# Global attention's sums of weights dealt out anew between VectorE and GpSimd, with the neighbourhood tables and the maxima placed differently

## The chip, the core and the metric

The kernel runs on one core of a Trainium2 chip. The core has engines with a queue each, worked off in order: TensorE (PE; matrix products into PSUM), VectorE (DVE), ScalarE (ACT), GpSimd (POOL) and SyncE (SP), which here issues the DMAs. The metric is the device time of one execution in microseconds. Most executions agree within 0.3%.

## What is computed

Two layers of a diffusion backbone on 1024 latent tokens (a grid of 16 rows by 64 columns) and 256 context tokens, width 1024, all in float32. Each layer: modulated norm, one input projection, three groups of heads, each multiplied by its own SiLU gate, one output projection and a gated residual. Cut to what matters here:

```python
def dense_attn(q, k, v):                       # global heads: 8 query heads, 2 key heads
    s = jnp.einsum("bqkgd,bskd->bkgqs", q, k)
    p = jax.nn.softmax(s, axis=-1)
    return jnp.einsum("bkgqs,bskd->bqkgd", p, v)
# neighbourhood heads (4): a query sees 8 rows x 16 columns around it, and the context
s = jnp.concatenate([s_nb + bias, s_ctx], axis=-1)
p = jax.nn.softmax(s, axis=-1)
o = einsum(p_nb, v_nb) + einsum(p_ctx, v_ctx)
y = jnp.concatenate([a_out * silu(ag), b_out * silu(bg), n_out * silu(ng)], -1) @ w_out
```

In the last layer only the latent tokens are queries; in the first the context tokens are too.

## The kernel before

**Stages.** Per layer: input projection (with norms, rotary embedding and gates, the results kept in DRAM), neighbourhood attention, in the first layer the context's own attention, global attention, output projection. The order of TensorE's instructions is the program's. Those of the other engines are set by a scheduler that runs at build time: each queue takes in order of the program what is ready by then, so a later step can come ahead of one that still waits. Once built, each queue is fixed.

**Neighbourhood attention** works in units of two heads and 128 queries: 8 units per pair of heads and layer, 10 in the first layer, and there 8 context units more (`units`, 28 in the first layer and 16 in the last). A unit has scores (L850, L851), the table of relative positions added and the minimum taken on DVE (L857), weights on ScalarE (L870), the gate times the reciprocal on POOL (`rg`, L873), transposes on TensorE (L886) through three PSUM banks `ps_b`, and values (L898). While unit n scores, unit n-1 transposes and unit n-2 takes its values. The table of a head exists twice: `ntab` (T, by DMA and L777), and `itab` (I), for inner queries: L781 copies ten columns of T, L782 to L784 overwrite its three outer pieces with a large number. There are two buffers of each, so heads 2 and 3 patch again what heads 0 and 1 patched. `before`, filled by `early(i, fn)`, says ahead of which unit a load is issued: the next pair's keys and queries, tables, the keys of the global attention (`gk`, three DMAs and two POOL memsets, L766 and L767) and its first queries (`load`).

**Global attention** has 8 units per layer (chunk of 512 queries, key head, pair of heads), `gunits`, numbered 0 to 7. Softmax needs each query's maximum first. `shift` makes it in 20 steps per unit: one product into a `ps_b` bank (L1007, or two of half the size, L1012) and its maximum on DVE (L1008, L1013); a 21st, `shift_rows`, puts the maxima into the second query operand. Of these steps 29 are done during the neighbourhood attention, from unit `nun - n_shifts` on, three a unit; the others run between the products of the global attention, one unit and a little ahead. For each unit and each kp from 0 to 4 (256 keys): scores of head hi=0, a shift step, the values of the step before, a shift step or two, scores of hi=1, two shift steps. Behind each group of scores stands the exponential on ScalarE into `gp` (L1036). The sum of weights of one head is a running sum `gacc` (L1041, L1044) over the five `gp`; the first three adds run on POOL, the last (kp=4) on DVE, and L1046 folds its two halves there. `finish` (at kp=2 of the next unit) sums over partitions on TensorE (L1062), makes the reciprocal (ScalarE L1066, L1067; DVE L1069, L1070), multiplies by gate and values (POOL L1071, DVE L1072), and `store_u` splits the result into a rounded part (`hh`, ScalarE's cast, L819) and the rest (`hl`, DVE, L820). `gp` and `gacc` share 7 buffers.

From unit 7 on, TensorE has no shift steps left: those of the last unit end in unit 6.

Of the kernel before, what the change touches and what calls it, by code (L numbers as in the profile page):

```python
# [7 lines left out]
F32 = mybir.dt.float32  # L8
F32R = mybir.dt.float32r
BF16 = mybir.dt.bfloat16  # L10
AF = mybir.ActivationFunctionType
ALU = mybir.AluOpType
# [4 lines left out]
P = 128  # L17
# [10 lines left out]
FAR = 1e30  # L28
# [46 lines left out]
def hybrid_block_kernel(  # L75
# [8 lines left out]
    PE, ACT, DVE, POOL, SP = nc.tensor, nc.scalar, nc.vector, nc.gpsimd, nc.sync  # L84
# [40 lines left out]
    def ps_one(name):  # L125
        wide.b += 1
        return ps_b[wide.b % 3]
# [250 lines left out]
    for l in range(DEPTH):  # L378
        last = l == DEPTH - 1
# [61 lines left out]
        def silu_to(dst, ps, n, s=None):  # L441
            s = s or wp.tile([P, 512], F32, name="sig", bufs=2)
            sigmoid(s[:, :n], ps)
            DVE.tensor_tensor(out=dst, in0=ps, in1=s[:, :n], op=ALU.mult)
# [48 lines left out]
        if l:  # L493
# [3 lines left out]
            for i in range(2):  # L497
                pr = ps_pair("ps_feat")
# [97 lines left out]
        for t in range(ntq):  # L596
            ps = proj_tok(W, t, 256)
            g = wp.tile([P, 512], F32, name="gate", bufs=2)
# [132 lines left out]
        def gate_out(ps, f, t0, n, s=None):  # L731
            g = s or wp.tile([P, 512], F32, name="gate", bufs=2)
            silu_to(g, ps, 512, s)
            SP.dma_start(out=agd[f, :, t0:t0 + n], in_=g)
# [15 lines left out]

        tab_bufs = [(ak_.tile([P, 14, 64], F32, name=f"ntab{i}"), ak_.tile([P, 10, 64], F32, name=f"itab{i}")) for i in range(2)]

        def kst():
            return ak_.tile([P, NT], F32R, name="kst", bufs=6)

# [6 lines left out]
        def load_gk(g):  # L762

            k1, k2 = load_twice(kst(), kad, g, 1), kst()
            SP.dma_start(out=k2[64:128].bitcast(F32), in_=head(kad, g, 0, slice(0, NT)))
            POOL.memset(k2[0:64].bitcast(F32), 0.0)  # L766
            POOL.memset(k2[0:1].bitcast(F32), 1.0)  # L767
            return k1, k2
# [9 lines left out]

        def na_inner(h):
            T, I = tab_bufs[h % 2]  # L780
            ACT.activation(out=I, in_=T[:, 2:12], func=AF.Copy)  # L781
            POOL.memset(I[0:64, 8:10], FAR)  # L782
            POOL.memset(I[64:128, 0:1], FAR)
            POOL.memset(I[64:128, 9:10], FAR)  # L784

        def load_nq(h, c0, n):
            t = ak_.tile([P, 512], F32R, name="nq", tag="q", bufs=QB)
# [13 lines left out]
        def na_q(pr, cc):  # L801
            cur["q", pr, cc] = [load_nq(2 * pr + hi, cc * 512, 512 if cc < 2 else 256) for hi in range(2)]
# [7 lines left out]
            g()  # L810


        def store_u(f, t0, n, u, eng=DVE):

            dst = hh[:, f, t0:t0 + n]
            if eng is POOL:
                POOL.tensor_copy(out=dst, in_=u)
            else:
                ACT.activation(out=dst, in_=u, func=AF.Copy)  # L819
            eng.tensor_tensor(out=hl[:, f, t0:t0 + n], in0=u, in1=dst.bitcast(F32), op=ALU.subtract)  # L820
# [86 lines left out]
        units, before = [], {}  # L907
# [3 lines left out]
        def early(i, fn):  # L911
            before.setdefault(max(i, 0), []).append(fn)

        order = [0, 1, 6, 7, 4, 5, 2, 3] + list(range(NTL, ntq))
        for pr in range(2):
            s0 = len(units)
            units += [("n", pr, t) for t in order]
            early(s0, lambda pr=pr: na_q(pr, 1))
            if not last:
                early(s0 + 4, lambda pr=pr: na_q(pr, 2))  # L920
            if pr == 0:
                for i, fn in enumerate(na_keys_load(1)):
                    early(s0 + 1 + i * (len(order) - 2) // 8, fn)
                for h in range(2):
                    early(s0 + 5 + h, lambda h=h: na_table(2 + h))
                early(len(units) - 1, lambda: na_q(1, 0))
                for h in range(2):
                    early(len(units) + 1 + h, lambda h=h: na_inner(2 + h))
            else:
                early(s0 + 4, lambda: gk(0))  # L930
        if not last:
            for g in range(2):
                for pr in range(2):
# [39 lines left out]
        def gk(g):  # L973
            if g not in gks:
                gks[g] = load_gk(g)
            return gks[g]


        def ga_unit(cc, g, pr):
            f = 2 * g + pr  # L980
            cs = slice(cc * 512, (cc + 1) * 512)
            st = _Env()
# [35 lines left out]
            def shift_rows():  # L1018
# [5 lines left out]
                for hi in range(2):  # L1024
                    SP.dma_start(out=st.q2[hi][0:1, :].rearrange("o (i p) -> o i p", p=P).bitcast(F32),
                                 in_=r[4 * hi:4 * hi + 4, :].bitcast(F32))

            def scores(hi, kp):
                k1, k2 = gk(g)
                S = ps_pair("ps_st").rearrange("p (a b) -> p a b", a=2)  # L1030
                for i in range(2):
                    kc = slice((2 * kp + i) * P, (2 * kp + i + 1) * P)
                    PE.matmul(S[:, i, :], k1[:, kc], st.q1[hi], start=True, stop=False)  # L1033
                    PE.matmul(S[:, i, :], k2[:, kc], st.q2[hi], start=False, stop=True)  # L1034
                p = ap_.tile([P, 2, 512], F32, name="gp", tag="prob", bufs=PB)
                ACT.activation(out=p, in_=S, func=AF.Exp)  # L1036
                st.p[hi, kp] = p
                pf = p.rearrange("p a b -> p (a b)")
                if kp == 1:
                    st.acc[hi] = ap_.tile([P, 1024], F32, name="gacc", tag="prob", bufs=PB)  # L1040
                    POOL.tensor_tensor(out=st.acc[hi], in0=st.p[hi, 0].rearrange("p a b -> p (a b)"), in1=pf, op=ALU.add)  # L1041
                elif kp > 1:
                    eng = DVE if kp == 4 else POOL
                    eng.tensor_tensor(out=st.acc[hi], in0=st.acc[hi], in1=pf, op=ALU.add)  # L1044
                if kp == 4:
                    DVE.tensor_tensor(out=st.acc[hi][:, 0:512], in0=st.acc[hi][:, 0:512], in1=st.acc[hi][:, 512:1024], op=ALU.add)  # L1046

            def values(kp, i):
                if kp == 0 and i == 0:
# [9 lines left out]
            def finish():  # L1059
                s_ps = ps_one("ps_gs")  # L1060
                for hi in range(2):
                    PE.matmul(s_ps[hi * 64:(hi + 1) * 64, :], ones, st.acc[hi][:, 0:512], start=True, stop=True)  # L1062
                gt = ap_.tile([P, 512], F32, name="ggate", tag="fin", bufs=4)
                SP.dma_start(out=gt, in_=agd[f, :, cs])
                r0 = ap_.tile([P, 512], F32, name="gr0", tag="fin", bufs=4)
                ACT.activation(out=r0, in_=s_ps, func=AF.Ln)  # L1066
                ACT.activation(out=r0, in_=r0, func=AF.Exp, scale=-1.0)  # L1067
                t1 = ap_.tile([P, 512], F32, name="gt1", tag="fin", bufs=4)
                DVE.tensor_tensor(out=t1, in0=s_ps, in1=r0, op=ALU.mult)  # L1069
                DVE.scalar_tensor_tensor(out=t1, in0=t1, scalar=-2.0, in1=r0, op0=ALU.add, op1=ALU.mult)  # L1070
                POOL.tensor_tensor(out=gt, in0=gt, in1=st.osb, op=ALU.mult)  # L1071
                DVE.scalar_tensor_tensor(out=t1, in0=t1, scalar=-1.0, in1=gt, op0=ALU.mult, op1=ALU.mult)  # L1072
                store_u(f, cc * 512, 512, t1)

            return shift, scores, values, finish, load, shift_rows

        gunits = [ga_unit(cc, g, pr) for cc in range(2) for g in range(2) for pr in range(2)]

        shifts = []
        for i, u in enumerate(gunits):  # L1080
# [1 line left out]
            shifts += own[:2] + ([gunits[i - 1][5]] if i else []) + own[2:]  # L1082
        shifts.append(gunits[-1][5])
        for i in range(2):
            early(len(units) - 12, gunits[i][4])

        use_banks("pair")
        env.att = False
# [3 lines left out]
        last_gate = 3, 512, 512  # L1092
        ps_gate = proj_feat(W, *last_gate, ps_acc)
# [3 lines left out]
        ap_ = attx.enter_context(pool(f"attp{l}", side=right))  # L1097
        prev = [None, None]
        nun = len(units)
        n_shifts = 7 if last else 10  # L1100
        n_ahead = 21 + GA_AHEAD

        def shift_step(n, least=0):
            for _ in range(n):
                if len(shifts) > least:
                    shifts.pop(0)()

        n_all = len(shifts)
        for n, u in enumerate(units + [None, None]):
            for fn in before.get(n, ()):  # L1110
                fn()
            fns = (make_unit(*u) if n else first) if u else None
            p1, p2 = prev
            for hi in range(2):
                if fns and n:
                    fns[0](hi)
                if p1:
                    p1[2](hi)
                if fns:
                    fns[1](hi)  # L1120
                if hi == 0 and n >= nun - n_shifts:
                    shift_step(1, n_all - n_ahead)
            shift_step(2 if n >= nun - n_shifts else 0, n_all - n_ahead)
            if n == 1:

                gate_out(ps_gate, *last_gate, tab_bufs[0][1].rearrange("p a k -> p (a k)")[:, 0:512])
            if p2:
                p2[3]()
            prev = [fns, p1]
            env.att = True  # L1130
# [38 lines left out]
        op = opx.enter_context(pool(f"op{l}", side=left))  # L1169
# [48 lines left out]
        for t0, n in ochunks:  # L1218
# [4 lines left out]
            for i in range(n):  # L1223
# [13 lines left out]
                elif last and t == NTL - 1:  # L1237

                    for c0, w in ((0, 512), (512, 256), (768, 256)):
                        ps, cs = ps_one("ps_y"), slice(c0, c0 + w)  # L1240
                        for k in range(KT):
                            a, b = hh[:, k, ts_], hl[:, k, ts_]
# [7 lines left out]
                else:  # L1250
                    ps, f = proj_out(t)
# [88 lines left out]
```

## Time and profile before

| what | us |
|---|---|
| median of the runs shown (3, from 1533.07 to 1533.96) | 1533.53 |
| profiled execution | 1532.11 |
| its span in the profile | 1530.3 |
| neighbourhood and context attention, first layer | 383 to 505 |
| global attention, first layer | 505 to 722 |
| neighbourhood attention, last layer | 1117 to 1219 |
| global attention, last layer | 1219 to 1436 |
| TensorE busy in the span | 1468.8 |

A row of the timeline has the start, the duration, engine, line, operation, out<-in, sizes and count; in brackets the time that the engine stood idle before it and what ended that. In a row of waits stand the waiting instruction, what it waited for, the total, how often and the longest. A row of stretches has for each engine the busy time and, in brackets, the instructions, in the order PE, PEld (weight loads), DVE, ACT, POOL, then the granted share of TensorE's clock, the share of the DMA engines, and GB/s.

### The profile page before, as it was taken

What the parts mean: (1) busy time and instruction counts of PE and PEld (TensorE: products, weight loads), DVE (VectorE), ACT (ScalarE), POOL (GpSimd) and SP (SyncE); (2) the same over time, 40 slices, a digit from 0 to 9 for tenths busy, and PEclk for the clock granted to TensorE, in tenths of its full rate; (3) what the DMA queues carried; (4) which work ended last, traced back from release to release, by engine and by line L of the source; (5) the groups of instructions that cost most, each with busy time, mean ns of one, the idle gap of its engine ahead of it and who ended that gap; (6) DMA issues with size and microseconds to landing.
All of it is one profiled execution on the core that took longest, in us unless ns stands there. A gap on an engine that the chain in (4) does not pass through costs nothing.

```text
span 1530.3 us, 22281 instructions
## 1 busy us (share of the span) xinstructions
PE 1468.8 (96%) x8001; PEld 1071.0 (70%) x8001; DVE 863.9 (56%) x1666; ACT 636.8 (42%) x1220; POOL 515.5 (34%) x630
## 2 busy tenths in 40 slices
PE   5999999999999999999999999999998999999999
PEld 3787777788887554544788888878787755544577
DVE  3545345542778678774533552464368878785522
ACT  4543232343776444444312452332466544444400
POOL 0243346000243565564001323460014265665300
PEclk9999999999999999999999999999999999999999
DMA  9447445437745101010522232343696201011331
GB/s 318 141 140 229 127 151 168 140 111 187 180 128 151 56 22 42 22 42 21 179 75 98 61 114 71 90 138 88 174 223 157 87 22 42 21 28 35 137 118 55
DMA packets 153040, 167.91 MB, mean 110 GB/s; under 512 B 35385, under 2 KB 112033, under 8 KB 152865
## 3 DMA queue, kind: packets, MB, share of 16 engines
q1 hardware_dynamic: 152928, 166.48, 37.0%
q8 instruction: 63, 1.03, 0.3%
q14 instruction: 49, 0.39, 0.1%
HBM read 126.45 MB, written 40.86 MB: 109 GB/s over the span
## 4 chain that ended last, share of the span: by engine, by line
PE 80%; DVE 8%; ACT 4%; DMA 4%; issue 3%; SPq 1%; POOL 0%; DVEq 0%; ACTq 0%; POOLq 0%
PE ps_c L1053 8%; PE ps_w L423 8%; PE ps_w L422 8%; PE ps_w L424 8%; PE ps_w L1208 4%; PE ps_w L1211 4%; PE ps_w L1209 4%; PE ps_w L1033 4%; PE ps_b L1007 4%; PE ps_c L898 3%; PE ps_w L1034 3%; PE ps_b L886 2%; PE ps_w L430 2%; PE ps_w L432 2%; PE ps_w L431 2%
## 5 line engine op out<-in xcount | busy, mean ns | idle before, releaser
L1036 ACT ACTIVATE gp<-ps_w 128x1024 f32<-128x1024 f32 x160 | 162.4, 1021 | 194.3 <-PE ps_w L1034 158.7
L422 PE MATMUL ps_w<-wh,hh 128*128 128x512 f32 (+1 forms) x624 | 234.7, 376 | 1.9 <-ACT wh L291 1.9
L423 PE MATMUL ps_w<-wl,hh 128*128 128x512 f32 (+1 forms) x624 | 228.6, 366 | 1.1 <-DVE wl L292 0.9
L424 PE MATMUL ps_w<-wh,hl 128*128 128x512 f32 (+1 forms) x624 | 228.1, 365 | 0.0
L1008 DVE TENSOR_REDUCE gmx<-ps_b 128x1 f32<-128x512 f32 x256 | 171.8, 685 | 73.5 <-PE ps_b L1007 69.3
L1053 PE MATMUL ps_c<-gp,av 128*64 128x512 f32 x640 | 169.3, 621 | 10.3 <-ACT gp L1036 10.3
L1044 POOL TENSOR_TENSOR gacc<-gacc,gp 128x1024 f32<-128x1024 f32 x64 | 161.3, 2547 | 25.8 <-ACT gp L1036 25.5
L422 PEld LDWEIGHTS ps_w<-wh,hh 128*128 128x128 f32 x624 | 117.7, 189 | 25.8 <-issue 2.9
L423 PEld LDWEIGHTS ps_w<-wl,hh 128*128 128x128 f32 x624 | 117.5, 188 | 21.8 <-DVE wl L292 2.8
L424 PEld LDWEIGHTS ps_w<-wh,hl 128*128 128x128 f32 x624 | 117.3, 188 | 21.1
L1034 PE MATMUL ps_w<-gq,kst 128*128 128x512 f32 x320 | 126.2, 395 | 0.0
L1208 PE MATMUL ps_w<-woh,hh 128*128 128x512 f32 x272 | 109.4, 402 | 0.0
L643 DVE TENSOR_REDUCE qss<-sq 128x8 f32<-128x512 f32 (+2 forms) x58 | 31.2, 538 | 136.2 <-ACT sq L641 136.2
L1209 PE MATMUL ps_w<-wol,hh 128*128 128x512 f32 x272 | 107.5, 395 | 0.0
L1053 PEld LDWEIGHTS ps_c<-gp,av 128*64 128x64 f32 x640 | 43.3, 138 | 89.4 <-issue 66.5
L1041 POOL TENSOR_TENSOR gacc<-gp 128x1024 f32<-128x1024 f32 x32 | 75.8, 2369 | 50.2 <-ACT gp L1036 50.2
L292 DVE TENSOR_TENSOR wl<-wraw,wh 128x512 fp32r<-128x512 f32 (+1 forms) x96 | 66.6, 713 | 37.4 <-ACT wh L291 35.9
L1211 PE MATMUL ps_w<-woh,hl 128*128 128x512 f32 x272 | 85.6, 395 | 0.0
L430 PE MATMUL ps_w<-hh,wh 128*128 128x512 f32 (+1 forms) x208 | 80.3, 386 | 1.3 <-ACT wh L291 1.3
L870 ACT ACTIVATE prob<-ps_w,m 128x768 f32<-128x768 f32 (+2 forms) x88 | 72.7, 826 | 20.6 <-DVE m L857 7.4
L432 PE MATMUL ps_w<-hh,wl 128*128 128x512 f32 (+1 forms) x208 | 78.6, 378 | 0.0
L431 PE MATMUL ps_w<-hl,wh 128*128 128x512 f32 (+1 forms) x208 | 78.0, 375 | 0.0
(225 smaller groups left out, 2914.8 us busy)
## 6 DMA issues: line engine op xcount, KB each, us to landing
wmod<-in_w_mod_dram SPq DMA_DIRECT2D x48, 512.0 KB
wraw<-in_w_in_dram SPq DMA_DIRECT2D x64, 256.0 KB
gq<-qad SPq DMA_DIRECT2D x64, 128.0 KB
woraw<-in_w_out_dram SPq DMA_DIRECT2D x14, 512.0 KB
wraw<-in_w_in_dram SPq DMA_DIRECT2D x48, 128.0 KB
kst<-knd SPq DMA_DIRECT2D x16, 320.0 KB
qad<-qklo SPq DMA_DIRECT2D x18, 256.0 KB
qad<-qkhi SPq DMA_DIRECT2D x18, 256.0 KB
```

The source lines that it names most:

```text
L422: PE.matmul(ps[:, :n], a, wh[:, off:off + n], start=(k == 0), stop=False)
L423: PE.matmul(ps[:, :n], a, wl[:, off:off + n], start=False, stop=False)
L424: PE.matmul(ps[:, :n], b, wh[:, off:off + n], start=False, stop=(k == KT - 1))
L430: PE.matmul(ps[:, :n], wh[:, fs], hh[:, k, ts_], start=(k == 0), stop=False)
L1008: DVE.reduce_max(out=mx[:, qt, half:half + 1], in_=S, axis=AX.X)
L1034: PE.matmul(S[:, i, :], k2[:, kc], st.q2[hi], start=False, stop=True)
L1036: ACT.activation(out=p, in_=S, func=AF.Exp)
L1044: eng.tensor_tensor(out=st.acc[hi], in0=st.acc[hi], in1=pf, op=ALU.add)
L1053: PE.matmul(st.o[hi * 64:(hi + 1) * 64, :], av[:, kt, g * 64:(g + 1) * 64], st.p[hi, kp][:, i, :], start=(kt == 0), stop=(kt == NTT - 1))
L1208: PE.matmul(ps[:, i2, :], a, oh[:, cs], start=(k == 0), stop=False)
L1209: PE.matmul(ps[:, i2, :], a, ol[:, cs], start=False, stop=False)
L1211: PE.matmul(ps[:, i2, :], b, oh[:, i2 * 512:(i2 + 1) * 512], start=False, stop=(k == KT - 1))
```

## The change

It has three parts.

*Who adds.* `add_eng` names the engine of each add of weights by unit n, head hi and kp. In units 0 to 5 the add of kp=4 stays on DVE for hi=0 and goes to POOL for hi=1, with its folding. In unit 6 DVE has the adds of kp=4 and that of hi=1, kp=3; in unit 7 it has all of hi=1 and kp=4 of hi=0. In units 5 and 6 `store_u` casts on DVE instead of ScalarE.

*Tables.* The outer pieces of both `itab` buffers are set once per layer, as the buffers are made, and `na_inner` copies the inner pieces alone, by two ScalarE instructions (64 partitions by 512 columns each). The last gate of the projection, which used the first `itab` as scratch, takes a tile of its own.

*Maxima.* The 29 early steps start at the 15th unit from the end instead of the 10th in the first layer (12th instead of 7th in the last), at two a unit instead of three (in the last layer two and three by turns). For that `gk(0)` is loaded ahead of unit 5 (first layer) or 3 (last) instead of unit 14 or 9 (there the first early step asks for it, ahead of the entry for unit 12), and the first two units' queries ahead of unit 11 or 2 instead of 16 or 4.

```diff
+        for T, I in tab_bufs:
+            POOL.memset(I[0:64, 8:10], FAR)
+            POOL.memset(I[64:128, 0:1], FAR)
+            POOL.memset(I[64:128, 9:10], FAR)
...
         def na_inner(h):
             T, I = tab_bufs[h % 2]
-            ACT.activation(out=I, in_=T[:, 2:12], func=AF.Copy)
-            POOL.memset(I[0:64, 8:10], FAR)
-            POOL.memset(I[64:128, 0:1], FAR)
-            POOL.memset(I[64:128, 9:10], FAR)
+            ACT.activation(out=I[0:64, 0:8], in_=T[0:64, 2:10], func=AF.Copy)
+            ACT.activation(out=I[64:128, 1:9], in_=T[64:128, 3:11], func=AF.Copy)
...
-        def store_u(f, t0, n, u, eng=DVE):
+        def store_u(f, t0, n, u, eng=DVE, cp=None):
             dst = hh[:, f, t0:t0 + n]
-            if eng is POOL:
-                POOL.tensor_copy(out=dst, in_=u)
+            if eng is POOL or cp:
+                (cp or eng).tensor_copy(out=dst, in_=u)
             else:
                 ACT.activation(out=dst, in_=u, func=AF.Copy)
...
-                early(s0 + 4, lambda: gk(0))
+                early(s0 - 5, lambda: gk(0))
...
+            def add_eng(hi, kp):
+                if n == 7:
+                    return DVE if hi or kp == 4 else POOL
+                if n == 6:
+                    return DVE if kp == 4 or (hi and kp == 3) else POOL
+                return DVE if kp == 4 and hi == 0 else POOL
...
                 if kp == 1:
-                    POOL.tensor_tensor(out=st.acc[hi], in0=st.p[hi, 0].rearrange("p a b -> p (a b)"), in1=pf, op=ALU.add)
+                    add_eng(hi, kp).tensor_tensor(out=st.acc[hi], in0=st.p[hi, 0].rearrange("p a b -> p (a b)"), in1=pf, op=ALU.add)
                 elif kp > 1:
-                    eng = DVE if kp == 4 else POOL
+                    eng = add_eng(hi, kp)
                     eng.tensor_tensor(out=st.acc[hi], in0=st.acc[hi], in1=pf, op=ALU.add)
                 if kp == 4:
-                    DVE.tensor_tensor(out=st.acc[hi][:, 0:512], in0=st.acc[hi][:, 0:512], in1=st.acc[hi][:, 512:1024], op=ALU.add)
+                    eng.tensor_tensor(out=st.acc[hi][:, 0:512], in0=st.acc[hi][:, 0:512], in1=st.acc[hi][:, 512:1024], op=ALU.add)
...
-                store_u(f, cc * 512, 512, t1)
+                store_u(f, cc * 512, 512, t1, cp=DVE if n in (5, 6) else None)
...
-            early(len(units) - 12, gunits[i][4])
+            early(max(len(units) - 17, 2), gunits[i][4])
...
-        n_shifts = 7 if last else 10
+        n_shifts = 12 if last else 15
...
-                if hi == 0 and n >= nun - n_shifts:
-                    shift_step(1, n_all - n_ahead)
-            shift_step(2 if n >= nun - n_shifts else 0, n_all - n_ahead)
+                if n >= nun - n_shifts:
+                    shift_step(1 + (hi and last and n % 2), n_all - n_ahead)
             if n == 1:
-                gate_out(ps_gate, *last_gate, tab_bufs[0][1].rearrange("p a k -> p (a k)")[:, 0:512])
+                gate_out(ps_gate, *last_gate, ap_.tile([P, 512], F32, name="fin", tag="fin", bufs=4))
```

More of the change, by code (lines that the diff above doesn't have):

```diff
@@ L976, in gk, with ga_unit @@
             return gks[g]
-        def ga_unit(cc, g, pr):
+        def ga_unit(n, cc, g, pr):
             f = 2 * g + pr
@@ L1072, in finish @@
                 DVE.scalar_tensor_tensor(out=t1, in0=t1, scalar=-1.0, in1=gt, op0=ALU.mult, op1=ALU.mult)
-                store_u(f, cc * 512, 512, t1)
+                store_u(f, cc * 512, 512, t1, cp=DVE if n in (5, 6) else None)
             return shift, scores, values, finish, load, shift_rows
-        gunits = [ga_unit(cc, g, pr) for cc in range(2) for g in range(2) for pr in range(2)]
+        gunits = [ga_unit(4 * cc + 2 * g + pr, cc, g, pr) for cc in range(2) for g in range(2) for pr in range(2)]
         shifts = []
```

## The prediction

> **What bounds the kernel now.** I read the page from the top (engines, then the chain), then the waits of TensorE by stage, then the timeline at the places where these waits end. PE is TensorE, DVE is VectorE, ACT is ScalarE, POOL is GpSimd.
>
> ```profile
> span 1530.3 us, 22281 instructions
> PE 1468.8 (96%) x8001; PEld 1071.0 (70%) x8001; DVE 863.9 (56%) x1666; ACT 636.8 (42%) x1220; POOL 515.5 (34%) x630
> PE 80%; DVE 8%; ACT 4%; DMA 4%; issue 3%; SPq 1%; POOL 0%; DVEq 0%; ACTq 0%; POOLq 0%
> ```
>
> TensorE is the bound: 96% busy and four fifths of the chain. The change takes no matmul away. It can only shorten or lengthen TensorE's waits, so what counts is each wait inside the two attention stages. In the second layer's global attention (1218 to 1438 us) the waits of TensorE are these two rows (us in total, times, longest); the first layer's come to the same within 0.1.
>
> ```profile
> PE ps_b L1007 <- DVE gmx L1008: 6.3, 6, 1.2
> PE ps_c L1053 <- ACT gp L1036: 5.1, 3, 3.1
> ```
>
> The first is one wait of 1.2 us at each boundary between two units, five per layer. The second is two large waits in the last two units. Here is the second of them in the timeline, then the granted clock (the column behind POOL) in the 3 us behind each, from the view of stretches.
>
> ```profile
> 1422.22 2.79 POOL L1044 TENSOR_TENSOR gacc<-gacc,gp 128x1024 f32<-128x1024 f32 x1
> 1422.91 2.65 DVE L1072 SCALAR_TENSOR_TENSOR gt<-gt,ggate 128x512 f32<-128x512 f32 x1
> 1425.60 0.63 ACT L819 ACTIVATE hh<-gt 128x512 fp32r<-128x512 f32 x1 [5.15 <-DVE gt L1072]
> 1426.13 1.92 ACT L1036 ACTIVATE gp<-ps_w 128x1024 f32<-128x1024 f32 x2
> 1427.19 3.51 PE L1053 MATMUL ps_c<-gp,av 128*64 128x512 f32 x6 [3.11 <-ACT gp L1036]
> ```
>
> ```profile
> 1400.00:1403.00 3.00, 3.00 (x7) 0.49 (x3) 2.33 (x1) 0.57 (x1) 2.14 (x1) 0.51 0.17 68
> 1427.00:1430.00 3.00, 2.81 (x6) 0.66 (x6) 1.85 (x1) 1.05 (x2) 2.34 (x1) 0.56 0.03 8
> ```
>
> Read it upwards: TensorE waits for an exponential, ScalarE runs it late because the cast L819 stands ahead of it in its queue, and the cast waits for DVE's L1072, which takes 2.65 us while POOL adds. Behind each of the two waits the clock was granted at 0.51 and 0.56.
>
> **The change, part by part.**
>
> *Last two units.* With the cast of finish 5 and finish 6 on DVE, ScalarE's queue no longer stands behind DVE; with the adds of the other half (hi=1) on DVE, POOL holds five adds in unit 6 and three in unit 7 where it held six. The waits of 5.1 us go, and with them the slow clock: 3 x 0.49 + 3 x 0.44 = 2.8 us. That is 7.9 us a layer. What is late next is DVE: cast, rest and up to five adds in unit 7, each 1.21 us alone (row of L1044 below), end about when the last values do. I take **8 us a layer, 16 in all**; from 6 (DVE's queue late by 2) to 9.5 (the shorter waits go too).
>
> *Units 0 to 5.* Here the add of hi=1, kp=4 and its folding move from DVE to POOL. The boundary of units 1 and 2 in the first layer, before:
>
> ```profile
> 552.29 1.21 DVE L1044 TENSOR_TENSOR gacc<-gacc,gp 128x1024 f32<-128x1024 f32 x1
> 552.78 1.02 ACT L1036 ACTIVATE gp<-ps_w 128x1024 f32<-128x1024 f32 x1 [1.48 <-PE ps_w L1034]
> 553.43 0.68 DVE L1008 TENSOR_REDUCE gmx<-ps_b 128x1 f32<-128x512 f32 x1
> 554.03 0.68 DVE L1046 TENSOR_TENSOR gacc<-gacc 128x512 f32<-128x512 f32 x1
> 554.16 0.50 PE L1007 MATMUL ps_b<-kst,hh 128*128 128x512 f32 x1 [1.25 <-DVE gmx L1008]
> 554.62 0.68 DVE L1008 TENSOR_REDUCE gmx<-ps_b 128x1 f32<-128x512 f32 x1
> 555.20 0.40 PE L1034 MATMUL ps_w<-gq,kst 128*128 128x512 f32 x1
> 555.23 1.21 DVE L1044 TENSOR_TENSOR gacc<-gacc,gp 128x1024 f32<-128x1024 f32 x1
> 555.44 0.42 PE L1012 MATMUL ps_b<-kst,hh 128*128 128x256 f32 x2
> ```
>
> The wait of 1.25 us ends with the maximum of 553.43, which stands behind the hi=0 add of 552.29. That add stays on DVE, and so does this wait. What goes, 555.23 and its folding, stands behind everything that TensorE waited for: its removal saves nothing. What comes is a collision. These rows show it:
>
> ```profile
> 560.56 1.02 ACT L1036 ACTIVATE gp<-ps_w 128x1024 f32<-128x1024 f32 x1 [0.36 <-PE ps_w L1034]
> 561.67 2.38 POOL L1041 TENSOR_TENSOR gacc<-gp 128x1024 f32<-128x1024 f32 x1 [1.92 <-ACT gp L1036]
> ```
>
> ```profile
> 1427.28 2.34 POOL L1044 TENSOR_TENSOR gacc<-gacc,gp 128x1024 f32<-128x1024 f32 x1 [2.27 <-ACT gp L1036]
> 1428.15 2.55 DVE L1044 TENSOR_TENSOR gacc<-gacc,gp 128x1024 f32<-128x1024 f32 x1 [1.20 <-ACT gp L1036]
> ```
>
> An idle POOL starts 0.09 us after the exponential's end (561.67 against 560.56 + 1.02). The moved add would start at 552.78 + 1.02 + 0.09 = 553.89 and hold POOL 2.34 us, to 556.23. And a DVE add with both inputs in SBUF that starts inside a POOL add waits for its end: 2.55 us instead of 1.21, ending 1.08 after POOL (1430.70 against 1429.62). The folding of hi=0 (554.03, both inputs in SBUF) starts 0.14 us after POOL would. It waits; L1072 above, also 512 wide, ended 0.55 after POOL (1425.56 against 1425.01), so the folding ends at 556.78 instead of 554.71. The maximum behind it ends at 557.4 instead of 555.30. Three ps_b banks go round, and L1012 at 555.44 needs the bank which this maximum frees: it starts at 557.4. **2.0 us more per boundary.** Layer 2 has nearly the same gap:
>
> ```profile
> 1374.19 1.02 ACT L1036 ACTIVATE gp<-ps_w 128x1024 f32<-128x1024 f32 x1 [1.48 <-PE ps_w L1034]
> ...
> 1375.42 0.68 DVE L1046 TENSOR_TENSOR gacc<-gacc 128x512 f32<-128x512 f32 x1
> ```
>
> POOL at 1375.30, the folding at 1375.42. Unit 0's boundary has no finish on DVE and its folding is over before the exponential, so five boundaries a layer, ten in all: **+20 us**. From below, nothing (the folding comes first: POOL waits 0.5 us and nobody waits for POOL). From above, the clock: after the change TensorE idles 1.25 us, works 1.44 (554.16 to 555.20 + 0.40), and idles 1.8 (to 557.4). An idle stretch of 1.86 us (next row) was followed by the 0.51 above, one of 1.25 never by a drop, and one of 2.6 in the neighbourhood attention by none (rows of the next part).
>
> ```profile
> 1399.71 0.79 PE L1053 MATMUL ps_c<-gp,av 128*64 128x512 f32 x2 [1.86 <-ACT gp L1036]
> ```
>
> So a drop of about 1.4 us (the mean of 3 x 0.49 and 3 x 0.44) may come at none or at all ten: 0 to 14 us. I take half, **+7 us**. [...]
>
> *Neighbourhood attention.* Patching the tables once takes POOL's memsets out of its queue. One of them blocked it:
>
> ```profile
> 1157.32 0.20 POOL L782 MEMSET itab<- 64x128 f32 x1 [3.12 <-ACT itab L781]
> ...
> 1157.89 0.61 POOL L873 TENSOR_SCALAR rg<-ngate,rr 128x64 f32<-128x64 f32 x2
> ```
>
> ```profile
> 1158.55 0.33 PE L886 MATMUL ps_b<-ident,rg 128*128 128x128 f32 x1 [2.62 <-POOL rg L873]
> ```
>
> ```profile
> 1158.00:1161.00 3.00, 2.45 (x33) 2.16 (x34) 1.75 (x4) 1.39 (x4) 1.57 (x8) 1.00 0.25 73
> ```
>
> That wait goes (2.6 us); in the first layer no such one is to be seen. The maxima at two a unit instead of three use the three banks less densely. All of TensorE's idle time there is the ceiling:
>
> ```profile
> 444.00:505.00 61.00, 57.41 (x527) 46.86 (x526) 49.87 (x134) 38.85 (x101) 25.44 (x72) 1.00 0.56 152
> 1139.00:1219.00 80.00, 73.80 (x731) 64.75 (x730) 65.37 (x160) 47.56 (x95) 24.79 (x63) 1.00 0.55 133
> ```
>
> 3.6 and 6.2 us, 2.6 of it named. Against it: the copy of the table as two ScalarE instructions, for which 0.6 us each stands near (the cast L819 has as many columns); ScalarE is busy 47.6 of 80 us, which hides it. The keys of gk(0) load six to nine units earlier and are needed five units earlier: three DMAs ahead of the table's and ngate's loads in SP's queue, and two POOL memsets ahead of rg. If they come at a bad place, one wait of 2.3 us.
>
> ```profile
> L766 POOL MEMSET kst<- x4: 1157/1160/1170, 370.4 to 1169.8; 64x1280 f32 x4
> L767 POOL MEMSET kst<- x4: 1154/1156/1162, 371.6 to 1171.1; 1x1280 f32 x4
> ```
>
> I take **-4 us**, from -8 to +2.
>
> *The rest.* Six memsets per layer at the opening of the pool, 1 us of POOL, beside the projection; the scratch of the last gate changes its tile: nothing.
>
> **The sum.** -16 + 20 + 7 - 4 = +7. The profiled execution took 1532.1 (span 1530.3 and 1.8 around it): 1539.1. The median of the runs shown is 1533.5, 1.4 above it, so I forecast **1540.5**.
>
> **The rivals.**
>
> *The folding wins (ends on the other side).* DVE starts the folding before POOL's add, because the scheduler puts it earlier or POOL starts 0.15 us later. Then boundaries cost nothing new and -16 - 4 = -20 stays: **1513.5**. For it: the gap is 0.14 and 0.12 us, and from that point the whole sum turns. Against it: the rows recur at all ten boundaries to a hundredth or two, and nothing ahead of the folding on DVE, POOL, ScalarE or TensorE is touched by the change. Chance 0.36. [...]
>
> *The folding loses, the clock holds.* -16 + 20 - 4 = 0: **1533.5**. For it: 2.6 us of idle time without a drop. Against it: 1.86 with one. Chance 0.12.
>
> *DVE's relief is worth more than I see.* With two instructions less, the scheduler orders DVE anew, the folding wins and the old 1.25 us go too: ten times 1.25 off 1513.5, **1501**. Chance 0.04; nothing in the rows puts the moved add ahead of the maximum.
>
> *The forecast itself*, folding blocked and the clock dropping in some boundaries: 0.48, with a range of its own from 1536 (two drops) to 1548 (all ten).
>
> **How the numbers follow.** Faster by over 0.2% (3 us, about what a measurement of this kernel can tell from no change): 0.36 + 0.04 = 0.40. Within: 0.12. Slower: 0.48. The range has to reach both sides: from 1509 (the folding wins, with part of the bounds of tail and neighbourhood) to 1548, which leaves out 1501 and the outermost ends.
>
> **What would show it.** The folding L1046 at some 2.7 us instead of 0.68 at ten boundaries, and L1012 waiting about 1.8 us for DVE's maximum: right; a mean of 0.7 for it: the first rival. The wait of L1053 for gp falls from 5.1 us to under 1 a layer, and the clock stays at 1.00 in the last two units: the tail is right. No wait of L886 for rg above 1 us: the table part. A clock of 0.5 just behind unit boundaries: the 7 us. The forecast is wrong if the scheduler orders DVE otherwise, or if POOL takes longer to start than it did.

## The result, and the profile after

The changed kernel takes 1551.7 us (median of 4 runs, 1550.7 to 1553.7) against 1533.3 for the kernel before: a ratio of 1.0128, 95% interval 1.0112 to 1.0144. It is 18 us slower. The forecast was 1540.5 with a range to 1548, so the sign was right and the size too small. The profiled execution has a span of 1548.9 us against 1530.3.

First the page's head, then the waits of TensorE in the second layer's global attention (1229 to 1455 us; total, times, longest), both of the changed kernel. L1011 and L1016 are the maxima's products (L1007 and L1012 before), L1065 the values (L1053), L1056 the add (L1044), L1058 the folding (L1046), L1074 the sums over partitions (L1062), L890 the transposes (L886), L877 `rg` (L873).

```profile
span 1548.9 us, 22273 instructions
PE 1475.8 (95%) x8001; PEld 1077.4 (70%) x8001; DVE 870.2 (56%) x1654; ACT 639.2 (41%) x1224; POOL 542.6 (35%) x634
...
PE 50%; DVE 10%; DMA 3%; issue 2%; ACT 2%; SPq 1%; POOL 0%; DVEq 0%; ACTq 0%
```

```profile
PE ps_b L1016 <- DVE gmx L1012: 9.5, 5, 1.9
PE ps_b L1011 <- DVE gmx L1012: 6.5, 6, 1.3
PE ps_b L1074 <- DVE gacc L1058: 0.8, 1, 0.8
PE ps_c L1065 <- ACT gp L1048: 0.2, 1, 0.2
```

The chain is followed back here only to 498 us (its shares add up to 68%), so they can't be laid beside those of the kernel before. The first experiment below, a1, without the moved add, is followed back as far (to 501 us): there DVE has 7% of the chain, here 10%, with 5 us more of busy time (870.2 against 865.5). DVE is hardly busier, it is later. The wait of 5.1 us for `gp` is down to 0.2, the old wait of 1.25 at each boundary is still there, and five waits of 1.9 are new. The first layer has the same rows within 0.3.

The timeline at the boundary of units 1 and 2 in the first layer, the place that the prediction worked through:

```profile
551.66 1.21 DVE L1056 TENSOR_TENSOR gacc<-gacc,gp 128x1024 f32<-128x1024 f32 x1
...
552.80 0.68 DVE L1012 TENSOR_REDUCE gmx<-ps_b 128x1 f32<-128x512 f32 x1
553.24 2.37 POOL L1056 TENSOR_TENSOR gacc<-gacc,gp 128x1024 f32<-128x1024 f32 x1 [2.06 <-ACT gp L1048]
...
553.40 2.76 DVE L1058 TENSOR_TENSOR gacc<-gacc 128x512 f32<-128x512 f32 x1
...
553.53 0.50 PE L1011 MATMUL ps_b<-kst,hh 128*128 128x512 f32 x1 [1.32 <-DVE gmx L1012]
...
554.56 0.40 PE L1046 MATMUL ps_w<-gq,kst 128*128 128x512 f32 x1
...
556.08 1.87 DVE L1012 TENSOR_REDUCE gmx<-ps_b 128x1 f32<-128x512 f32 x3
...
556.81 0.80 PE L1016 MATMUL ps_b<-kst,hh 128*128 128x256 f32 x2 [1.85 <-DVE gmx L1012]
```

GpSimd's moved add starts at 553.24 and the folding 0.16 us later. The folding takes 2.76 us instead of 0.68, ends 0.55 after the add, and the maximum behind it ends at 556.76, where TensorE has waited for it. The prediction had 0.14 for the gap, 0.55 for the end and a wait of about 1.8.

The clock, from the view of stretches (length, then PE, PEld, DVE, ACT, POOL busy, the granted clock, DMA share, GB/s). The first row is the stretch that holds the second wait of the next boundary (587.18 to 589.04); the first wait, of 1.32 us, ended before it, at 585.75. The others are the stretches behind four boundaries:

```profile
587.00:590.40 3.40, 1.54 (x9) 0.66 (x10) 3.40 (x5) 1.02 (x1) 2.43 (x2) 1.00 0.19 66
590.40:593.80 3.40, 3.40 (x11) 1.60 (x8) 1.07 (x2) 0.60 (x1) 0.83 (x1) 0.50 0.00 0
...
621.10:624.50 3.40, 3.40 (x10) 1.42 (x7) 0.99 (x2) 0.60 (x1) 0.48 (x1) 0.51 0.00 0
651.90:655.30 3.40, 3.40 (x10) 1.17 (x6) 0.82 (x3) 0.60 (x1) 0.20 (x1) 0.50 0.00 0
682.60:686.00 3.40, 3.40 (x11) 1.10 (x8) 0.86 (x2) 0.50 (x1) 0.00 (x0) 0.50 0.00 0
```

Half the clock behind each of them. Nine of the ten boundaries have it; the one behind 556.3 us lasts for two stretches, so there are ten half-clock stretches. The stretch ahead holds the second wait alone in four cases, 1.86 us, and in five (the one of 552.87 to 556.28 among them) parts of both, 1.98 us. The boundary without one is the second layer's first:

```profile
1279.90:1283.30 3.40, 1.65 (x8) 0.78 (x10) 3.40 (x5) 0.96 (x1) 2.14 (x2) 1.00 0.09 34
1283.30:1286.80 3.50, 3.50 (x17) 2.23 (x13) 1.94 (x4) 1.63 (x2) 1.29 (x1) 1.00 0.00 0
```

TensorE was idle for 1.75 us of that stretch against 1.86 of the one from 587.00.

Where the 18.6 us come from, by the starts of TensorE's first instruction of each stage and unit in both traces (us; the tail is unit 6 and 7 from the first score of each to the last value, and the way from there to the output projection):

| part | forecast | found |
|---|---|---|
| boundaries in units 2 to 6: stall | +20 | +22 |
| boundaries: clock | +7 | +15 |
| tail, both layers | -16 | -18.4 |
| neighbourhood and context stages (122.0 to 120.8, 100.2 to 101.3) | -4 | -0.1 |
| a half-clock stretch at 501.7, where the first layer's global attention begins | 0 | +0.7 |
| the rest of the program | 0 | -0.5 |

The boundaries' 37 is the difference of the global attention between the changed kernel (227.8 and 223.4) and the first experiment (207.5 and 206.9), which differs there alone. Another experiment below, a3, divides it: its profile has every stall and no half-clock stretch, and its units 2 to 6 take 21.9 us more than a1's and 14.9 less than the changed kernel's (both layers, from unit to unit).

### The profile page after: what moved, and what is told of

Same layout as the page of the kernel before. It is cut to its first block, busy times and chain, and to the rows that moved or that the text cites. A ratio compares the mean times of both kernels' runs of the same rounds, so it can differ in the third digit from the quotient of the medians.

```text
span 1548.9 us, 22273 instructions
## 1 busy us (share of the span) xinstructions
PE 1475.8 (95%) x8001; PEld 1077.4 (70%) x8001; DVE 870.2 (56%) x1654; ACT 639.2 (41%) x1224; POOL 542.6 (35%) x634
## 4 chain that ended last, share of the span: by engine, by line
PE 50%; DVE 10%; DMA 3%; issue 2%; ACT 2%; SPq 1%; POOL 0%; DVEq 0%; ACTq 0%
PE ps_c L1065 8%; PE ps_w L1218 4%; PE ps_w L1221 4%; PE ps_w L1219 4%; PE ps_w L1045 4%; PE ps_w L423 3%; PE ps_w L1046 3%; PE ps_w L424 3%; PE ps_w L422 3%; PE ps_b L1011 3%; DVE gmx L1012 2%; DVE gacc L1058 2%; DVE gacc L1056 2%; PE ps_b L1016 1%; DVE gt L1084 1%
## 5 line engine op out<-in xcount | busy, mean ns | idle before, releaser
L1012 DVE TENSOR_REDUCE gmx<-ps_b 128x1 f32<-128x512 f32 x256 | 170.1, 685 | 78.6 <-PE ps_b L1011 75.0
L1056 POOL TENSOR_TENSOR gacc<-gacc,gp 128x1024 f32<-128x1024 f32 x70 | 175.1, 2524 | 50.3 <-ACT gp L1048 50.0
L1065 PE MATMUL ps_c<-gp,av 128*64 128x512 f32 x640 | 170.6, 641 | 0.3 <-ACT gp L1048 0.3
L1046 PE MATMUL ps_w<-gq,kst 128*128 128x512 f32 x320 | 127.3, 398 | 0.0
L877 POOL TENSOR_SCALAR rg<-ngate,rr 128x64 f32<-128x64 f32 x88 | 28.6, 328 | 226.1 <-DVE m L861 95.2
L1065 PEld LDWEIGHTS ps_c<-gp,av 128*64 128x64 f32 x640 | 45.3, 142 | 76.7 <-issue 67.6
L1053 POOL TENSOR_TENSOR gacc<-gp 128x1024 f32<-128x1024 f32 x30 | 71.1, 2370 | 52.1 <-ACT gp L1048 52.1
```

What stands on the lines that cost most here:

```text
L1012: DVE.reduce_max(out=mx[:, qt, half:half + 1], in_=S, axis=AX.X)
L1065: PE.matmul(st.o[hi * 64:(hi + 1) * 64, :], av[:, kt, g * 64:(g + 1) * 64], st.p[hi, kp][:, i, :], start=(kt == 0), stop=(kt == NTT - 1))
```

## The experiments

Each starts from the changed kernel unless it says otherwise; all are timed beside the kernel before.

| run | median us | ratio to before, 95% |
|---|---|---|
| a1_last_add_back | 1516.6 | 0.9895 (0.9881 to 0.9910) |
| a2_fold_pool | 1513.6 | 0.9876 (0.9859 to 0.9893) |
| a3_scores_twice | 1537.0 | 1.0021 (1.0007 to 1.0035) |
| d1_fold_first | 1513.5 | 0.9874 (0.9848 to 0.9900) |
| b4_cast_alone | 1525.9 | 0.9951 (0.9930 to 0.9973) |
| b5_adds_alone | 1527.7 | 0.9965 (0.9950 to 0.9980) |
| b2_tables_alone | 1532.3 | 0.9990 (0.9974 to 1.0005) |
| b3_maxima_alone | 1532.9 | 1.0003 (0.9986 to 1.0020) |
| a4_mirror | 1502.6 | 0.9799 (0.9780 to 0.9818) |
| a4_again | 1499.2 | 0.9780 (0.9759 to 0.9801) |
| c1_mirror_old_maxima | 1502.5 | 0.9796 (0.9773 to 0.9818) |
| e1_mirror_only_sums | 1504.1 | 0.9806 (0.9785 to 0.9827) |

**Is it the moved add?** One line back:

```diff
-                return DVE if kp == 4 and hi == 0 else POOL
+                return DVE if kp == 4 else POOL
```

> The changed kernel, with the last add of hi=1 and its folding back on VectorE in units 0 to 5; tail, tables and maxima as changed. Theory: the ten boundaries with a blocked folding carry the whole loss, 37 us (units 2 to 6 of each layer, with the clock), so the time falls to about 1514.5, the folding takes 0.68 us each time and no half clock is left at boundaries. Rival (the spread maxima or the tail's adds set the boundaries off): over 1535.

1516.6, 2 above the expectation; the new waits and the half-clock stretches at boundaries are gone, and units 1 to 5 take 27.1 us each, as before the change. So this line carries 35 us (1551.7 - 1516.6), and everything else in the change together gains 17 (1533.3 - 1516.6).

**Is it the collision, or GpSimd's load?** The moved add stays; the folding of hi=0 goes to GpSimd as well, which gives it one folding more per unit than the change does:

```diff
-                    eng.tensor_tensor(out=st.acc[hi][:, 0:512], ...
+                    (POOL if n < 6 else eng).tensor_tensor(out=st.acc[hi][:, 0:512], ...
```

> The changed kernel, with the folding of hi=0 on GpSimd too in units 0 to 5, so that VectorE has no instruction with two SBUF inputs inside the moved add. Theory (the folding is blocked by the moved add): the stall of 1.85 us and the clock drops go although GpSimd has more work than ever, about 1514.5, within 3. Rival (a busier GpSimd is what costs): 1552 or more. Second rival (GpSimd's queue becomes too long and the sums come late to the finish): between, 1520 to 1540, with TensorE waiting for gacc.

1513.6. More work on GpSimd (busy for 552.5 us against 542.6), 38 us less: its load is not what costs, and no wait for the sums is new.

**Is it who starts first?** Both stay where the change has them, the add on GpSimd and the folding on VectorE, but the add is held back until the folding is over:

```diff
+                    if n < 6 and hi and kp == 4:
+                        z = small.tile([P, 1], F32, tag="gz", name="gz")
+                        POOL.tensor_scalar(out=z, in0=st.acc[0][:, 0:1], scalar1=0.0, scalar2=None, op0=ALU.mult)
+                        POOL.tensor_tensor(out=st.acc[1][:, 0:1], in0=st.acc[1][:, 0:1], in1=z, op=ALU.add)
```

> The changed kernel with the moved add still on GpSimd and the folding of hi=0 still on VectorE, but two GpSimd instructions of one column ahead of the add, the first of which reads the folded sum: so the add can start only when the folding is over. Theory (what decides is which of the two starts first, and the add is harmless if it is second): the folding takes 0.68 us again and the time falls to about 1514.5, as with the add back on VectorE. Rival (an add of 2.3 us on GpSimd at this place holds VectorE up in any case, its maxima too): 1530 to 1552.

1513.5. The timeline of this kernel at the same boundary (here L1060 is the add, L1062 the folding):

```profile
555.75 0.68 DVE L1062 TENSOR_TENSOR gacc<-gacc 128x512 f32<-128x512 f32 x1
555.88 0.19 PEld L1011 LDWEIGHTS ps_b<-kst,hh 128*128 128x128 f32 x1 [1.73 <-DVE gmx L1012]
555.88 0.50 PE L1011 MATMUL ps_b<-kst,hh 128*128 128x512 f32 x1 [1.30 <-DVE gmx L1012]
...
556.35 1.88 DVE L1012 TENSOR_REDUCE gmx<-ps_b 128x1 f32<-128x512 f32 x3
...
556.52 0.21 POOL L1058 TENSOR_SCALAR gz<-gacc 128x1 f32<-128x1 f32 x1 [2.98 <-DVE gacc L1062]
...
557.08 2.36 POOL L1060 TENSOR_TENSOR gacc<-gacc,gp 128x1024 f32<-128x1024 f32 x1
...
557.15 0.43 PE L1016 MATMUL ps_b<-kst,hh 128*128 128x256 f32 x2
```

The add starts 1.33 us after the folding where it stood 0.16 ahead of it, and with the same work on the same engines (and 24 tiny instructions more) the program is 38 us faster. The folding ends at 556.43, ahead of the add, so the two no longer overlap: what costs is the overlap, and not the add itself. Which of two that do overlap is held is seen elsewhere, in the changed kernel above and in a4 below. The maxima of 556.35 read PSUM: the second and the third run beside the add, and the three take 0.63 us each (1.88 / 3), against 0.68 for the single one of 552.80 above. At this boundary of the changed kernel the folding, with both inputs in SBUF, was held (2.76 us), and the three maxima behind it, the first two beside GpSimd's folding (555.69 to 557.28), took 0.62 us each (1.87 / 3).

**What part is the clock?** The first scores of units 2 to 6 are computed twice; the second result replaces an equal one. TensorE has more to do, inside its stall:

```diff
+                    for _ in range(2 if 2 <= n <= 6 and kp == 0 and hi == 0 else 1):
                         PE.matmul(S[:, i, :], k1[:, kc], st.q1[hi], start=True, stop=False)
                         PE.matmul(S[:, i, :], k2[:, kc], st.q2[hi], start=False, stop=True)
```

> The changed kernel, in which the first scores of units 2 to 6 (four matmuls, 0.93 us) are computed twice, inside the stall of 1.85 us at the boundary: more work for TensorE, less idle time in a row. Theory (a drop of the clock follows when TensorE is idle for some 1.85 us within 3.4): the ten half-clock stretches go and the stall stays, about 1.7 us off each: 1534.5, within 3. Rival (the loss beyond the stall is no matter of the clock but of a longer chain): 1551.7 up to 1561, nine tenths of a us more at each of ten boundaries.

1537.0 (1532.7 to 1539.2 in ten runs), the profiled execution 1533.9: 15 us less than the changed kernel for 9 us more of matrix products. The row of the wait in this kernel, and its first layer's global attention in one stretch, with the clock at 1.00:

```profile
556.22 0.51 PE L1016 MATMUL ps_b<-kst,hh 128*128 128x256 f32 x2 [0.96 <-DVE gmx L1012]
```

```profile
505.00:722.00 217.00, 205.16 (x849) 108.88 (x847) 158.09 (x193) 96.83 (x114) 141.48 (x63) 1.00 0.10 30
```

No half-clock stretch is left in either layer of this profile, while the folding is still blocked and TensorE goes on as late as before: the units are 29.3 us long, as long as the one unit of the changed kernel with a stall and no drop (29.30). This separates the two parts of the loss in the profiles: 15 us clock, 22 us stall. The median shows the same 15 us (1551.7 - 1537.0), though some half clock remains in other executions: in five of the ten the mean granted clock is 0.995 or 0.996 (1536.5 to 1539.2 us), and where it fell there is not known.

**The tail: cast or adds?** The kernel before with one of them each.

```diff
-                store_u(f, cc * 512, 512, t1)
+                store_u(f, cc * 512, 512, t1, cp=DVE if cc and f in (1, 2) else None)
```

> The kernel before with the cast of finish 5 and finish 6 on VectorE alone; all adds as before. Theory: ScalarE's queue no longer stands behind VectorE, so the two waits of 5.1 us a layer and the two half-clock stretches go without any add moved: global attention 216.6 down to some 208 a layer, time about 1517. Rival (VectorE itself is late, blocked by GpSimd's adds, and the adds have to move too): the waits move to the sums and half or less is gained, 1525 or more.

1525.9, between theory and rival. The stage itself falls as the theory says, to 206.8 a layer; but then the sums of unit 7 are late. Two rows of this kernel, VectorE's cast behind GpSimd's adds and TensorE's second wait for the sums (L1062):

```profile
709.62 2.48 DVE L817 CAST hh<-gt 128x512 fp32r<-128x512 f32 x1
...
717.67 1.70 PE L1062 MATMUL ps_b<-gacc,ones 128*64 128x512 f32 x2 [1.85 <-DVE gacc L1046]
```

From the last value to the output projection it now takes 6.4 and 6.7 us instead of 1.7.

```diff
+            def add_eng(hi, kp):
+                if cc and f == 3:
+                    return DVE if hi or kp == 4 else POOL
+                if cc and f == 2:
+                    return DVE if kp == 4 or (hi and kp == 3) else POOL
+                return DVE if kp == 4 else POOL
...
-                    eng = DVE if kp == 4 else POOL
+                    eng = add_eng(hi, kp)
```

> The kernel before with the adds of units 6 and 7 dealt out as changed, the cast still on ScalarE, units 0 to 5 untouched. Theory: part of the 5.1 us stays, since the cast still waits for VectorE's product behind GpSimd's remaining adds, but it shortens: 1520 to 1530. Rival (the adds are all that matters): 1517, as with everything.

1527.7: the waits for `gp` shrink from 5.1 to 3.7 us a layer, longest 1.9, and one half-clock stretch a layer stays. Alone the two parts gain 6 and 4.5 us. No run has just the two together; by the starts of unit 6 and of the output projection in the profiles, the tails of both layers are 9.9 us shorter with the cast alone, 6.3 with the adds alone, and 18.4 in a1, which has both. The cast opens ScalarE's queue, the adds let VectorE finish the sums in time; either alone gains a part and leaves a wait.

**Tables and maxima**, each alone on the kernel before:

> The kernel before with the table part alone (outer pieces set once, two copies on ScalarE, own scratch tile). Theory: the wait of 2.6 us for rg in the second layer goes and nothing else moves, so the second layer's neighbourhood stage falls from 100.2 to about 97.5 us and the time by 2 to 3 us (1530.5). Rival (the wait is for something else, the gate's DMA or the reciprocal, and only moves): 100.2 as before, 1533.5.

> The kernel before with the maxima part alone (early steps thinner and sooner, keys and queries loaded sooner). Theory: it gives back in the second layer what the tables gain (loads crowd the gate's DMA ahead of rg, two new waits of 1.5 and 0.7 us) and gains about 1 us in the first: stages of about 120.5 and 102.5 to 103.5 us against 122.0 and 100.2, time 1533 to 1536. Rival (the maxima part is the gain and the tables do nothing): second stage under 99, time about 1530.

Both came out at no change in time. In the stages more can be seen. The first layer's takes 119.6 to 120.9 us in the eight profiles with the new maxima and 121.8 to 122.4 in the six with the old ones, whatever the tables: there the maxima gain about 2 us. The second layer's takes 102.9 us in b3, as that expectation said, but b4 has 103.1 with the old maxima, so that they give it back there is not shown.

The tables' wait of 2.6 us for `rg` in the middle of the second layer's stage is there in the kernel before and in b4, b5 and e1, 2.9 with the maxima alone, and in no kernel with the new tables: that cause is shown. But with the tables alone other rows took its place (TensorE's waits in that stage of b2, whose L889 and L1010 are the transposes and a maximum's product):

```profile
PE ps_b L889 <- DMA ngate<-ngd: 2.0, 1, 2.0
PE ps_b L1010 <- DVE gmx L1011: 1.9, 1, 1.9
PE ps_b L1015 <- ACT probt L894: 1.3, 1, 1.3
```

The wait for the maximum was 0.7 before (1.9 in c1 too, which has the new tables with the old maxima). The wait behind the gate's load, 10 to 12 us into the stage, is between 0.4 and 2.0 us in the fourteen profiles (that it is the load's is read in the row of b2, and only inferred in kernels whose row names `rg`), and kernels with the same code there differ as much as others. And the old wait of 2.6 has a price that the kernel before did not happen to show. Here are two stretches of b4, which has the old tables; the wait ends in the first:

```profile
1155.00:1158.30 3.30, 1.41 (x23) 1.29 (x25) 2.28 (x4) 2.73 (x5) 1.47 (x8) 1.00 0.07 20
1158.30:1161.70 3.40, 3.40 (x23) 3.07 (x20) 1.13 (x4) 0.00 (x0) 1.35 (x4) 0.50 0.74 189
```

A half-clock stretch follows it in b3, b4 and b5, in before and e1 none; what decides it is not shown. So the second layer's stage takes 100.2, 103.1, 101.8 and 100.2 us in before, b4, b5 and e1, which have the same code there.

**The other way round.** From the boundary's rows: the old 1.25 us came of VectorE's add of hi=0 ahead of the maximum. So GpSimd takes hi=0 and VectorE hi=1:

```diff
-                return DVE if kp == 4 and hi == 0 else POOL
+                return DVE if kp == 4 and hi == 1 else POOL
```

> The changed kernel with the heads exchanged in units 0 to 5: GpSimd takes the last add and folding of hi=0, VectorE those of hi=1. Theory: the old wait of 1.25 us came of VectorE's hi=0 add ahead of the maximum; with that add on GpSimd both it and the blocked folding are gone, about 1514.5 - 12.5 = 1502. Rival (VectorE's other instructions with two SBUF inputs, L824 or the add of hi=1, are blocked in their turn and hold the maxima up): 1520 or more.

1502.6, 31 us faster than before and 49 faster than the change. Units 1 to 5 take 25.95 us instead of 27.13, and TensorE waits for no maximum in the global attention. VectorE and GpSimd at the same boundary, in the second profile of this kernel:

```profile
546.11 1.67 DVE L824 TENSOR_TENSOR hl<-gt,hh 128x512 fp32r<-128x512 f32 x1
547.70 2.47 DVE L1012 TENSOR_REDUCE gmx<-ps_b 128x1 f32<-128x512 f32 x4
...
550.10 1.21 DVE L1056 TENSOR_TENSOR gacc<-gacc,gp 128x1024 f32<-128x1024 f32 x1
550.11 2.33 POOL L1058 TENSOR_TENSOR gacc<-gacc 128x512 f32<-128x512 f32 x1
```

Four maxima run in a row, 0.62 us each (2.47 / 4), while GpSimd adds, and VectorE's add comes behind them. L824 is held, as the rival said (1.67 us against 0.69 in a1), but no maximum comes too late by it. Here VectorE starts 0.01 us ahead, and it is GpSimd that is held: its folding takes 2.33 us instead of 1.29 (as in d1), and nobody waits for it.

Last, how much tables and maxima are worth in this kernel: it runs again, then with the maxima as before, then with the tables as before too (the edits are the diff of the change, undone).

> The mirrored kernel a second time, beside its two variants: 1502.5 as the first time, neighbourhood stages of 120.1 and 101.3 us.

> The mirrored kernel (hi=0 to GpSimd) with the early maxima and the loads placed as before the change. If the maxima part is worth its 1 to 2 us (first layer's stage 120 against 122), this is slower than a4_again by as much, 1504; if the second layer gives it back, the same.

> The kernel before with the mirrored sums and the tail's part alone: tables and maxima as before. If these two parts are worth nothing together, 1502.5; if they are worth the 4 us that were forecast, 1506.5.

1499.2 (1496.7 to 1502.0), 1502.5 (1499.1 to 1505.4) and 1504.1 (1501.0 to 1506.0), five runs each; the two neighbourhood stages together 220.8, 221.2 and 222.6 us. By the medians both parts together gain 1.5 to 5 us against the two times of the mirrored kernel (1502.6, 1499.2), but the runs overlap, and the gate's load moves the stage by as much. What the tables alone are worth stays open.

## Why the prediction was right or wrong

**What bounds the kernel**: right. Nearly all of the loss and the gain lies in waits of TensorE inside the attention stages and in the half clock behind them; matrix products did not change.

**The collision** (+20, found +22): right in each step. Gap 0.16 us for 0.14, folding 2.76 us for 2.75, stall 1.85 at ten boundaries, and the second layer's one boundary without a clock drop made its unit 29.30 us long instead of 27.14: 2.16 for the 2.0. With the folding first, d1 gave 1513.5, the number of the first rival. In the changed kernel and in a4 the one that started second was held: VectorE's folding (2.76 us for 0.68) by an add that started 0.16 us ahead, and GpSimd's folding (2.33 us for 1.29) by VectorE's add that started 0.01 us ahead.

**The clock** (+7, found +15): this is the step that failed. The prediction had a drop at none or at all ten boundaries, 0 to 14 us, and wrote "I take half". With 7 for the 15 the time would have been 1544, inside the range.

The price of a drop was about right: 1.4 us was forecast. The second layer's units of 30.75 and 29.30 us, with a half-clock stretch and without, differ by 1.45; against the units of a3 a drop costs 1.4 us in the second layer and 1.6 in the first. Half of a stretch of 3.41 us would be 1.7. The second layer's half-clock stretches begin while TensorE still waits (3.09 us busy in the one from 1310.63); the four of the first layer that are shown above are busy all through.

The number was wrong: not half, but nine of ten boundaries, one with two stretches. Ten even chances were the wrong picture, since the boundaries of a layer are not independent: in both layers the drop, once there, came back at each later boundary (the last section says why it could).

Could the first drop have been foreseen? The half-clock stretches are 3.41 us long, and they begin whole multiples of that apart (in the changed kernel 556.28 and 1310.63 us: 221 times 3.413; in the kernel before 686.70 and 1400.08 us: 209 times), so I counted idle time by stretches laid out from their starts. Idle time of 1.85 or 1.86 us in one was followed by a drop in the kernel before and the changed one, 1.75 by none. But the bound is not sharp. In b3, TensorE waited for 1.88 us in one stretch, and the next had the full clock; in the kernel before, the equal wait at the same place, of which 1.85 us lay in one stretch, was followed by a drop at 686.7. The stretch of b3 and the one behind it:

```profile
682.43:685.84 3.41, 1.53 (x6) 0.37 (x6) 1.88 (x2) 2.19 (x3) 1.14 (x2) 1.00 0.93 339
685.84:689.25 3.41, 3.41 (x15) 1.67 (x12) 3.01 (x2) 1.11 (x2) 1.85 (x1) 1.00 0.07 28
```

In the stretch ahead of the drop at 501.7 us in the changed kernel TensorE was idle for 1.52 us. And it need not be one wait: in the stretch of 552.87 to 556.28, ahead of the first drop at a boundary, it was idle for 0.66 and 1.32 us. Take the boundary worked through above: idle from 552.21 to 553.53, at work to 554.96, idle to 556.81. If 1.85 us is enough, a stretch of 3.41 us holds it wherever it begins between 552.08 and 554.96, that is for 2.88 / 3.41 = 84% of its positions; if it takes 1.9, for 40% (552.13 to 553.48). So the first drop of a layer was between 40 and 84%, an estimate from such bounds, and half was no bad guess for it; what could have been seen is that it might repeat, since 27.1 + 2.0 + 1.4 = 30.5 us is near nine stretches (30.7). What else decides a drop stays open.

The upper end of 1548 had all ten drops in it and still fell short by 3.7 us. It made no allowance for the neighbourhood's 4 us, which did not come; the stall's 2 us more and the tail's 2.4 us less nearly cancel.

**The tail** (-16): right, slightly too small (-18.4). The waits for `gp` fell to 0.2 and the clock is 1.00 there. What was said to be late next, VectorE, is: TensorE waits 0.8 us for the last sum. b4 and b5 show that each of the two moves gains only a part of it; the forecast took them as one step.

**Neighbourhood attention** (-4): not borne out. The named wait went, as said, but between the two profiles the gain is 0.1: the first layer gains 1.2 us and the second loses 1.1. By the prediction's own sign, no wait for `rg` above 1 us, the table part did not come out either: 1.5 us of such a wait remain, at another place. The stage varies too much from one execution to the next for two profiles to carry a term of this size; part of what hid it here was that wait for the gate's load (1.5 us in the changed kernel's profile, 0.4 in that of before).

**The rivals**: "the clock holds" (1533.5) is what a3 comes near to, at 1537.0. That d1 met the first rival's 1513.5 to the microsecond is in part luck: its sum had -16 and -4 where -18.4 and -0.1 were found. That the old 1.25 us could go as well was priced at 1501, and the mirrored kernel reached it (1502.6, 1499.2), but not with this change: the add of hi=0 has to leave VectorE, not that of hi=1.

## What to carry to other kernels

Before work is dealt out anew between VectorE and GpSimd, look at which instruction of VectorE starts just behind the new GpSimd instruction, and who waits behind it: here a folding with both inputs in SBUF that started 0.16 us after an add took 2.76 us for 0.68, and the program 38 us more than in d1. Move the work that stands ahead of what the bottleneck waits for, not the work behind it. And where a stall of TensorE recurs, add up its idle time over 3.41 us, the length of a half-clock stretch here, and see whether its period is near a whole number of such stretches: here, at 30.75 us for nine (30.72), one drop was followed by one at each later boundary of the layer, so that the chance of a drop was that of all of them together.

## What the runs showed of the hardware

A unit with the stall and a half-clock stretch takes 30.75 us in the second layer (30.9 in the first), which is nine stretches of 3.41 us (30.72): the next boundary falls on nearly the same place of the stretch again, TensorE is idle for the same 1.86 us in each of the four stretches ahead, and a drop, once there, came back at each boundary to the end (590.4, 621.1, 651.9, 682.6 us). The second layer's first boundary had no drop; its unit of 29.30 us shifted the next boundary, and from there on all had one (1310.6, 1341.4, 1372.1, 1402.8 us).

A plain cast of VectorE, with one input, was also held by GpSimd's adds: 2.48 us in b4 against 0.43 for the same cast in a1.

The half clock behind 556.3 us lasted 6.8 us where the others of that profile lasted 3.4. Other profiles have such pairs too, and in the attention stages of all fourteen they go together with idle time in the first of the two: it was idle for 0.53 us here and for 0.75, 1.20 and 1.27 in b2 and b4, and no half-clock stretch that was followed by the full clock was idle for more than 0.38. A pair at 27.2 us of e1, outside these stages, had none, so the cause stays open.
